# Hybrid decoder layer: spatial layer norm placed behind the recurrence's chunks, branch splits behind the value evictions

## Chip, cores and metric

The kernel runs on one core of one Trainium2 chip. The metric is the device time of one execution in microseconds. The kernel before takes 758.96 us, the median of 3 runs (758.95 to 759.19).

## The reference, cut to what matters

One decoder layer on x (512 tokens, 1024 channels). An RMS norm is followed by one wide input projection w_in whose columns feed three token mixers, their gate paths and the merge gates. The mixers are a sparse attention (NSA), a chunked spatial-gating MLP and an RWKV-7 recurrence. Each mixer's output is multiplied by a SiLU gate, projected from 512 to 1024 channels, scaled by a sigmoid merge gate and summed; an output projection, a gated per-layer embedding and a last RMS norm follow. Everything is float32. The two parts that the change touches:

```python
def _spatial_gating(u, v, ln_g, ln_b, w_s, b_s):
    vn = ((vf - mu) * lax.rsqrt(var + LN_EPS)) * ln_g + ln_b      # layer norm of v over 512 channels
    mixed = einsum('gts,bcsgd->bctgd', tril(w_s), vn) + b_s       # 8 groups, chunks of 128 tokens
    return u * mixed

ys = stack([y_nsa * silu(nz), y_sg * silu(sz), y_rk * silu(rz)])  # the three finished branch outputs
zs = einsum('bsnc,ncd->bsnd', ys, w_branch)
x = x + sum(sigmoid(mg) * zs) @ w_o
```

The recurrence (`_rwkv7`) carries a 64 x 64 state for each of 8 heads over the 512 tokens.

## The kernel before, in words

**Projections in three products.** Each float32 operand of a projection is split into a high part (rounded to the matmul's reduced float32 type) and a low part, and a product is made of three matmuls: high by high, high by low, low by high. `wload` (L66 to L79) brings one piece of weights: a DMA on SP's queue into wr (L75, 4 buffers), a cast on ScalarE into the high half wh (L77, 5 buffers), a subtraction into the low half wl (L78, 5 buffers). The engine of that subtraction is what `ph_["l"]` holds, VectorE or GpSimd, and is set from place to place. A piece holds at most 560 elements per partition, so a block of 128 columns by 1024 rows takes 2 pieces, 256 columns take 4. `fm_block` (L149) makes one block of 128 output features for all 512 tokens, 24 matmuls with 512 columns; `tm_chunk` (L159) makes up to 512 features for four tiles of 128 tokens. Both put their result into the PSUM tile mm_ps, which has two banks (L58), and call an eviction function.

**Order of the work.** The kernel is written as one list; a scheduler of the framework then puts every engine's instructions into an order of its own, by the program's order as priority and by its own timeline of the kernel, and each engine works its list off in that order. `tc.issue_after(ins)` adds an edge: the instructions of the block that run on the engine of `ins` stand behind `ins` in that engine's list. The projections that don't depend on the mixers (su, sv, merge gates, sz, rz, nz) are so laid between the steps of the mixers.

**The recurrence** (L536 to L605) goes over 8 chunks of 64 tokens. In each chunk TensorE makes r_ps from the state SV, ScalarE copies it, TensorE makes u_ps, VectorE and ScalarE copy it into SV (L557, L558), TensorE makes the state update s_ps (st_ps in the trace), VectorE adds and scales it into tn (L567, or L569 and L570) and VectorE and ScalarE copy tn into the next chunk's SV (L572, L573). The next chunk's r_ps reads that. Every second chunk a group norm of the outputs follows (L582 to L605).

**Spatial gating** (L641 to L689). su and sv have been stored to device memory by then. The norm's parameters lng and lnb, the spatial weights, us and vn (sv's tiles) are loaded on SP's queue; for each of four tiles VectorE runs bn_stats and bn_aggr (L665, L666); the inverse deviation rs4 comes from VectorE and GpSimd (L668, L669); then for each tile VectorE subtracts and scales (L671), GpSimd multiplies with lng (L672), VectorE adds lnb (L673). Eight mixing matmuls (mx_ps), the gate product with sz, and four transposes give y1, which is stored to device memory (L689).

**Branch outputs and NSA's projections.** After rz and nz (L691 to L701), y1 is loaded (zs, L724) and split into ysH and ysL by `split` (L715: ScalarE L716, VectorE L717); for y2 the recurrence's output vt is joined with rz (zs, L729; L730) and split in the same way. Then come the projections of NSA: values and gate for four tiles (`ev_v`, L743 to L749: L745 ScalarE, L746 VectorE, L747 ScalarE, L748 VectorE), four query blocks (`ev_q`, L752) and two key blocks (`ev_k`, L761). The attention and the merges (L775) follow; merge 1 is the first to read y1. The merge's tiles (pool gp, L772) take over memory that is released when y2 is done.

```python
    def split(h, l, src, sc):
        S.activation(h, src, AF.Copy, scale=sc)
        V.scalar_tensor_tensor(l, src, sc, f(h), op0=OP.mult, op1=OP.subtract)
```

Of the kernel before, what the change touches and what calls it, by code (L numbers as in the profile page):

```python
# [9 lines left out]
F32 = mybir.dt.float32  # L10
# [21 lines left out]
CH = {("nz", 3): 7, ("nz", 2): 5}  # L32
LV = (("su", 0), ("su", 1), ("sv", 0), ("sv", 1))
C0 = math.exp(-0.5)

# [4 lines left out]
def f(ap):  # L40
    return ap.bitcast(F32)
# [3 lines left out]
def hybrid_kernel(ctx, tc, x, p, norm_g, w_in, cmp_w1, cmp_w2, cmp_pe, sg_ln_g, sg_ln_b, sg_w, sg_b,  # L45
# [489 lines left out]

    canch = []  # L536
    own = [slice(0, 64), slice(64, 128)]
    for c in range(8):
# [20 lines left out]
        if c < 7:  # L559
            s_ps = rps.tile([128, 4, 64], F32, tag="ch", name="st_ps", bufs=2)  # L560
            for q in range(4):
                for e in range(2):
                    mm(s_ps[own[e], q, :], BKt[:, c, q, e, :], SV[:, c, e, q, :], True, True)
            tn = iv.tile([128, 4, 64], F32, tag="tn", name="tn", bufs=2)
            dbc = Dt[:, :, c:c + 1].to_broadcast([128, 4, 64])
            if c == 0:
                V.tensor_tensor(tn, s_ps, dbc, OP.mult)  # L567
            else:
                V.tensor_tensor(tn, s_ps, sn, OP.add)  # L569
                V.tensor_tensor(tn, tn, dbc, OP.mult)  # L570
            sn = tn
            V.tensor_copy(SV[own[0], c + 1, 0], tn[own[0]])  # L572
            S.copy(SV[own[1], c + 1, 1], tn[own[1]])  # L573
# [45 lines left out]
    for m in range(NG):  # L619
# [5 lines left out]
        with ExitStack() as es:  # L625
            if ("sg", m) in CH:
                es.enter_context(tc.issue_after(canch[CH["sg", m]]))
            fm_block(O_MG + 1024 + m * 128, 128, ev_m)

    for nm, off in (("sz", O_SZ),):  # L630
        for hf in range(2):
            def ev_t(t, ps, nm=nm, hf=hf):
# [6 lines left out]
                SY.dma_start(dr[nm][t * 128:(t + 1) * 128, hf * 256:hf * 256 + 256], st[:, 0:256])  # L639
            tm_chunk([(w_in, off + 256 * hf, 256)], hH, hL, 8, ev_t)  # L640
    sg_ctx = ExitStack()  # L641
    sp = sg_ctx.enter_context(tc.tile_pool(name="sp", bufs=2))
# [17 lines left out]
    for t in range(4):  # L660
        rows = slice(t * 128, (t + 1) * 128)
        SY.dma_start(us[:, t, :], dr["su"][rows, :])
        SY.dma_start(vn[:, t, :], dr["sv"][rows, :])
        bs = sp.tile([128, 6], F32, tag="bs", name="bs", bufs=1)
        V.bn_stats(bs, vn[:, t, :])  # L665
        V.bn_aggr(mv[:, t, :], bs)  # L666
    rs4 = sp.tile([128, 4], F32, tag="rs4", name="rs4", bufs=1)
    V.tensor_scalar(rs4, mv[:, :, 1], 1e-5, None, op0=OP.add)  # L668
    G.tensor_tensor(rs4, rs4, mhalf[:, 0:4], OP.pow)  # L669
    for t in range(4):  # L670
        V.tensor_scalar(vn[:, t, :], vn[:, t, :], mv[:, t, 0:1], rs4[:, t:t + 1], op0=OP.subtract, op1=OP.mult)  # L671
        G.tensor_tensor(vn[:, t, :], vn[:, t, :], lng, OP.mult)  # L672
        V.tensor_tensor(vn[:, t, :], vn[:, t, :], lnb, OP.add)  # L673
    for g in range(8):
# [43 lines left out]

    zp_ctx = ExitStack()
    zp = zp_ctx.enter_context(tc.tile_pool(name="zp", bufs=4))  # L720
    y1H, y1L = ytiles()
    for q in range(4):
        zs = zp.tile([128, 512], F32, tag="z", name="zs")
        SY.dma_start(zs, dr["y1"][q * 128:(q + 1) * 128, :])  # L724
        split(y1H[:, q, :], y1L[:, q, :], zs, 0.5)
    y2H, y2L = ytiles()
    for q in range(4):
        zs = zp.tile([128, 512], F32, tag="z", name="zs")
        SY.dma_start(zs, dr["rz"][q * 128:(q + 1) * 128, :])  # L729
        V.scalar_tensor_tensor(vt[:, q, :], vt[:, q, :], pc("lnx_b", q), zs, op0=OP.add, op1=OP.mult)  # L730
        split(y2H[:, q, :], y2L[:, q, :], vt[:, q, :], 0.5)
    zp_ctx.close()
    kp_ctx.close()


# [3 lines left out]
    kst = [nsa.tile([128, 2, 2, 512], R, name=f"kst{b}") for b in range(2)]  # L739
    vst = nsa.tile([128, 4, 2, 2, 128], R, name="vst")  # L740
    gate = nsa.tile([128, 4, 24], F32, name="gate")

    def ev_v(t, ps):  # L743
        pv = ps[:, 0:256].rearrange("p (b g d) -> p b g d", b=2, g=2)
        S.copy(vst[:, t, :, :, 0:64], pv)  # L745
        V.tensor_tensor(vst[:, t, :, :, 64:128], pv, f(vst[:, t, :, :, 0:64]), OP.subtract)  # L746
        S.activation(gate[:, t, :], ps[:, 256:280], AF.Tanh, scale=0.5)  # L747
        V.tensor_scalar(gate[:, t, :], gate[:, t, :], 0.5, 0.5, op0=OP.mult, op1=OP.add)  # L748
    tm_chunk([(w_in, O_NVS, 128), (w_in, O_NVW, 152)], hH, hL, 8, ev_v)  # L749

    for q in range(4):
        def ev_q(ps, q=q):  # L752
            S.activation(qst[0:64, q, 0, :], ps[0:64], AF.Copy, scale=0.125)
            S.activation(qst[64:128, q, 1, :], ps[64:128], AF.Copy, scale=0.125)
            V.scalar_tensor_tensor(qst[64:128, q, 0, :], ps[0:64], 0.125, f(qst[0:64, q, 0, :]),
                                   op0=OP.mult, op1=OP.subtract)
            V.scalar_tensor_tensor(qst[0:64, q, 1, :], ps[64:128], 0.125, f(qst[64:128, q, 1, :]),
                                   op0=OP.mult, op1=OP.subtract)
        fm_block(O_NQ + 128 * q, 128, ev_q)
    for b in range(2):  # L760
# [8 lines left out]
        fm_block((O_NKS, O_NKW)[b], 128, ev_k)  # L769


    gp = ctx.enter_context(tc.tile_pool(name="gp", bufs=2))  # L772
# [224 lines left out]
```

## Time and profile before

| what | value |
|---|---|
| time of the runs, median (lowest to highest) | 758.96 us (758.95 to 759.19) |
| time of the profiled execution | 758.88 us |
| its span from the first to the last instruction | 757.1 us |
| mean granted TensorE clock | 0.989 |
| ScalarE busy | 353.7 us |
| GpSimd busy | 327.6 us |
| DMA | 78.73 MB, mean 104 GB/s |

The profile names engines in short: PE is TensorE's matmuls, PEld its weight loads, DVE VectorE, ACT ScalarE, POOL GpSimd, SP the queue of SyncE. The granted clock is a share of 2.4 GHz. Idle time of an engine is put down to what ended it last. In rows of a timeline the first number is the start, the second the duration, both in us, and the bracket is the idle time ahead of it with its releaser.

### The profile page before, as it was taken

How to read it: one execution, taken by the hardware profiler on the slowest of the kernel's cores; microseconds unless marked ns; L12 is line 12 of the kernel's file. 1: busy time of each engine (PE TensorE's matmuls, PEld its weight loads, DVE VectorE, ACT ScalarE, POOL GpSimd, SP SyncE). 2: the span in 40 equal slices, each digit the busy share in tenths (PEclk: the TensorE clock that was granted, in tenths of full speed). 3: DMA queues.
4: the chain of work that ended last, by engine and by line, in shares of the span. 5: the costliest groups of instructions: out<-in, count | busy, mean ns of one | idle time of the engine just before them, and what ended most of it. 6: DMA issues, size and time to landing. Idle time of an engine off the chain costs nothing.

```text
span 757.1 us, 13075 instructions
## 1 busy us (share of the span) xinstructions
PE 720.5 (95%) x4941; PEld 610.3 (81%) x4941; DVE 403.1 (53%) x747; ACT 353.7 (47%) x743; POOL 327.6 (43%) x304
## 2 busy tenths in 40 slices
PE   4999999999996999999899999989999999999995
PEld 4888788899875987778777777867877888998995
DVE  6531688658817553456558456387655222216335
ACT  6454565533351332334464655476654333127453
POOL 6455731020335343424534335533445656256563
PEclk9999999999998999999999999999999999999999
DMA  5853222234553353346434222211117433222222
GB/s 197 186 142 85 64 73 59 72 97 118 147 171 111 100 165 112 103 140 182 138 84 125 57 56 56 71 29 42 43 47 250 121 98 110 72 98 75 79 70 112
DMA packets 106689, 78.73 MB, mean 104 GB/s; under 512 B 5569, under 2 KB 97282, under 8 KB 106626
## 3 DMA queue, kind: packets, MB, share of 16 engines
q1 hardware_dynamic: 105890, 75.27, 34.6%
q10 hardware_dynamic: 736, 2.63, 0.8%
q8 instruction: 39, 0.64, 0.3%
q14 instruction: 24, 0.20, 0.1%
HBM read 67.91 MB, written 9.96 MB: 103 GB/s over the span
## 4 chain that ended last, share of the span: by engine, by line
PE 83%; DVE 6%; DMA 3%; ACT 3%; issue 2%; POOL 1%; SPq 0%; ACTq 0%; POOLq 0%; DVEq 0%
PE mm_ps L61 66%; PE s_ps L61 3%; PE o_ps L61 2%; PE g_ps L61 2%; PE p_ps L861 2%; PE Yp L61 1%; DMA vn<-dr_sv 1%; DMA lnb<-in_sg_ln_b_dram 1%; PE r_ps L61 1%; DVE mx L847 1%; PE mx_ps L61 1%; DVE vn L671 1%; DVE pl L865 1%; ACT wh L77 1%; DMA zs<-dr_y 1%
## 5 line engine op out<-in xcount | busy, mean ns | idle before, releaser
L78 POOL TENSOR_TENSOR wl<-wr,wh 128x512 fp32r<-128x512 f32 (+1 forms) x168 | 225.0, 1348 | 292.8 <-ACT wh L77 279.1
L77 ACT CAST wh<-wr 128x512 fp32r<-128x512 f32 (+1 forms) x194 | 119.1, 620 | 162.7 <-PE mm_ps L61 112.3
L61 PE MATMUL mm_ps<-hH,wh 128*128 128x512 f32 (+1 forms) x440 | 174.9, 397 | 5.7 <-ACT gate L747 2.8
L61 PE MATMUL mm_ps<-hL,wh 128*128 128x512 f32 (+1 forms) x440 | 172.9, 393 | 0.0
L61 PE MATMUL mm_ps<-hH,wl 128*128 128x512 f32 (+1 forms) x440 | 172.2, 392 | 0.0
L61 PEld LDWEIGHTS mm_ps<-hH,wh 128*128 128x128 f32 x440 | 83.9, 191 | 24.0 <-ACT gate L747 3.5
L61 PEld LDWEIGHTS mm_ps<-hH,wl 128*128 128x128 f32 x440 | 83.8, 191 | 17.9 <-DVE wl L78 0.3
L61 PEld LDWEIGHTS mm_ps<-hL,wh 128*128 128x128 f32 x440 | 84.0, 191 | 16.7 <-issue 0.2
L61 PE MATMUL mm_ps<-wh,hL 128*128 128x256 f32 (+1 forms) x224 | 65.3, 292 | 0.0
L61 PE MATMUL mm_ps<-wl,hH 128*128 128x256 f32 (+1 forms) x224 | 64.7, 289 | 0.0
L61 PE MATMUL mm_ps<-wh,hH 128*128 128x256 f32 (+1 forms) x224 | 64.3, 289 | 0.0
L61 PEld LDWEIGHTS mm_ps<-wh,hH 128*128 128x128 f32 x224 | 42.8, 192 | 1.3 <-issue 0.5
L61 PEld LDWEIGHTS mm_ps<-wh,hL 128*128 128x128 f32 x224 | 43.0, 192 | 0.9 <-issue 0.5
L61 PEld LDWEIGHTS mm_ps<-wl,hH 128*128 128x128 f32 x224 | 42.9, 191 | 0.8
L865 DVE TENSOR_TENSOR pl<-p_ps,ph 128x512 fp32r<-128x512 f32 x40 | 27.1, 684 | 26.8 <-ACT ph L864 26.7
L61 PE MATMUL mm_ps<-ysH,wh 128*128 128x512 f32 x96 | 38.6, 402 | 0.2 <-ACT ysH L716 0.2
L61 PE MATMUL mm_ps<-ysL,wh 128*128 128x512 f32 x96 | 38.4, 400 | 0.2 <-DVE ysL L717 0.2
L61 PE MATMUL mm_ps<-ysH,wl 128*128 128x512 f32 x96 | 38.2, 398 | 0.0
L848 ACT ACTIVATE P<-s_ps,mx 128x512 f32<-128x512 f32 (+3 forms) x64 | 33.4, 532 | 7.8 <-DVE mx L847 5.5
L61 PE MATMUL mm_ps<-wh,mH 128*128 128x256 f32 x128 | 36.1, 286 | 0.6 <-DVE x L910 0.6
L61 PE MATMUL mm_ps<-wl,hT 128*128 128x256 f32 x128 | 35.8, 281 | 0.0
L61 PE MATMUL mm_ps<-wl,mH 128*128 128x256 f32 x128 | 35.8, 281 | 0.0
(336 smaller groups left out, 1437.1 us busy)
## 6 DMA issues: line engine op xcount, KB each, us to landing
wr<-in_w_in_dram SPq DMA_DIRECT2D x130, 256.0 KB
wr<-in_w_branch_dram SPq DMA_DIRECT2D x24, 256.0 KB
wr<-in_w_o_dram SPq DMA_DIRECT2D x16, 256.0 KB
wr<-in_w_ple_gate_dram SPq DMA_DIRECT2D x16, 256.0 KB
xs__129<-in_x_dram SPq DMA_DIRECT2D x4, 512.0 KB
w1t<-in_cmp_w_dram SPq DMA_DIRECT2D x4, 512.0 KB
x<-in_x_dram ACTq DMA_DIRECT2D x4, 512.0 KB
out_dram<-x SPq DMA_DIRECT2D x8, 256.0 KB
```

The lines of the kernel that those rows point to most:

```text
L61: return PE.matmul(o, a, b, start=start, stop=stop, **kw).ins
L77: S.copy(h[:, :m], raw[:, :m])
L78: ph_["l"].tensor_tensor(l[:, :m], raw[:, :m], f(h[:, :m]), OP.subtract)
L671: V.tensor_scalar(vn[:, t, :], vn[:, t, :], mv[:, t, 0:1], rs4[:, t:t + 1], op0=OP.subtract, op1=OP.mult)
L847: V.tensor_reduce(mx[:, hh:hh + 1], s_ps[:, :W], axis=AX.X, op=OP.max, negate=True)
L848: S.activation(P[:, hh, :W], s_ps[:, :W], AF.Exp, bias=mx[:, hh:hh + 1], accum_out=sm[:, hh:hh + 1])
L861: PE.transpose(p_ps[:, hh * 128:hh * 128 + 128], P[:, hh, kt * 128:kt * 128 + 128], ident)
L865: V.tensor_tensor(pl, p_ps, f(ph), OP.subtract)
```

## The change

`vanch` collects VectorE's last state copy of each chunk 0 to 6 (L572). With LA = 1, bn_stats and bn_aggr of all four tiles stand behind chunk 1's copy on VectorE, the norm of tiles 0 and 1 behind chunk 2's, that of tiles 2 and 3 behind chunk 3's. The multiplication with lng moves from GpSimd to VectorE. The low halves of sz's weights, and those of the NSA values, queries and keys, are made on VectorE in place of GpSimd. The loads and splits of y1 and y2 move behind the NSA projections in the program; on ScalarE and VectorE y1's stand behind the gate instructions of value tile 3, and y2's behind the evictions of query blocks 0 (for q = 0, 1) and 1 (for q = 2, 3).

```diff
+LA = 1
-    canch = []
+    canch, vanch = [], []
-            V.tensor_copy(SV[own[0], c + 1, 0], tn[own[0]])
+            vanch.append(V.tensor_copy(SV[own[0], c + 1, 0], tn[own[0]]).ins)
+    ph_["l"] = V
     for nm, off in (("sz", O_SZ),):
...
+    ph_["l"] = G
...
-        V.bn_stats(bs, vn[:, t, :])
-        V.bn_aggr(mv[:, t, :], bs)
+        with tc.issue_after(vanch[LA]):
+            V.bn_stats(bs, vn[:, t, :])
+            V.bn_aggr(mv[:, t, :], bs)
...
-        V.tensor_scalar(vn[:, t, :], vn[:, t, :], mv[:, t, 0:1], rs4[:, t:t + 1], op0=OP.subtract, op1=OP.mult)
-        G.tensor_tensor(vn[:, t, :], vn[:, t, :], lng, OP.mult)
-        V.tensor_tensor(vn[:, t, :], vn[:, t, :], lnb, OP.add)
+        with tc.issue_after(vanch[LA + 1 + t // 2]):
+            V.tensor_scalar(vn[:, t, :], vn[:, t, :], mv[:, t, 0:1], rs4[:, t:t + 1], op0=OP.subtract, op1=OP.mult)
+            V.tensor_tensor(vn[:, t, :], vn[:, t, :], lng, OP.mult)
+            V.tensor_tensor(vn[:, t, :], vn[:, t, :], lnb, OP.add)
...
-    (loads and splits of y1 and y2: from here)
+    nanch = []
+    ph_["l"] = V
...
-        S.activation(gate[:, t, :], ps[:, 256:280], AF.Tanh, scale=0.5)
-        V.tensor_scalar(gate[:, t, :], gate[:, t, :], 0.5, 0.5, op0=OP.mult, op1=OP.add)
+        a_ = S.activation(gate[:, t, :], ps[:, 256:280], AF.Tanh, scale=0.5).ins
+        nanch.append((a_, V.tensor_scalar(gate[:, t, :], gate[:, t, :], 0.5, 0.5, op0=OP.mult, op1=OP.add).ins))
...
+    (ev_q appends its second activation and its last VectorE instruction to nanch in the same way)
...
+    y1H, y1L = ytiles()
+    for q in range(4):
+        zs = zp.tile([128, 512], F32, tag="z", name="zs")
+        SY.dma_start(zs, dr["y1"][q * 128:(q + 1) * 128, :])
+        with tc.issue_after(nanch[3][0]), tc.issue_after(nanch[3][1]):
+            split(y1H[:, q, :], y1L[:, q, :], zs, 0.5)
+    y2H, y2L = ytiles()
+    for q in range(4):
+        zs = zp.tile([128, 512], F32, tag="z", name="zs")
+        SY.dma_start(zs, dr["rz"][q * 128:(q + 1) * 128, :])
+        with tc.issue_after(nanch[4 + q // 2][0]), tc.issue_after(nanch[4 + q // 2][1]):
+            V.scalar_tensor_tensor(vt[:, q, :], vt[:, q, :], pc("lnx_b", q), zs, op0=OP.add, op1=OP.mult)
+            split(y2H[:, q, :], y2L[:, q, :], vt[:, q, :], 0.5)
+    zp_ctx.close()
+    kp_ctx.close()
+    ph_["l"] = G
```

## Rows read from the trace of the kernel before

**Rows 1.** The page, busy us of each engine, share of the span, instructions.

```profile
PE 720.5 (95%) x4941; PEld 610.3 (81%) x4941; DVE 403.1 (53%) x747; ACT 353.7 (47%) x743; POOL 327.6 (43%) x304
```

**Rows 2.** Waits of PE over the span: us in total, times, longest.

```profile
PE r_ps L61 <- DVE SV L572: 3.3, 1, 3.3
PE st_ps L61 <- DVE SV L557: 3.2, 1, 3.2
PE mm_ps L61 <- ACT gate L747: 2.8, 2, 2.0
```

**Rows 3.** Windows: length, busy PE, PEld, DVE, ACT, POOL, granted clock, DMA share, GB/s.

```profile
227.40:230.60 3.20, 0.01 (x1) 0.00 (x0) 1.89 (x5) 0.00 (x0) 0.00 (x0) 1.00 0.71 263
230.60:234.90 4.30, 4.25 (x38) 3.56 (x39) 2.49 (x7) 1.47 (x3) 1.54 (x2) 0.61 0.42 135
237.30:240.60 3.30, 0.02 (x1) 0.03 (x1) 3.27 (x5) 1.02 (x3) 3.30 (x4) 1.00 0.16 55
240.60:245.40 4.80, 4.80 (x51) 4.53 (x51) 3.62 (x5) 1.25 (x3) 4.05 (x2) 0.64 0.14 55
353.50:362.20 8.70, 5.90 (x26) 4.45 (x25) 8.70 (x10) 5.24 (x13) 6.48 (x5) 1.00 0.67 177
```

**Rows 4.** Timeline of DVE, 227 to 240 us.

```profile
227.44 0.69 DVE L665 BATCH_NORM_STATS2 bs<-vn 128x6 f32<-128x512 f32 x1 [10.27 <-DMA vn<-dr_sv]
...
230.20 0.40 DVE L557 COPY SV<-u_ps 64x256 f32<-64x256 f32 x1
...
232.11 0.69 DVE L665 BATCH_NORM_STATS2 bs<-vn 128x6 f32<-128x512 f32 x1 [0.36 <-DMA vn<-dr_sv]
...
234.42 4.78 DVE L671 TENSOR_SCALAR vn<-vn,mv,rs 128x512 f32<-128x512 f32 x4 [1.20 <-POOL rs L669]
239.11 0.41 DVE L567 TENSOR_TENSOR tn<-st_ps,Dt 128x256 f32<-128x256 f32 x1
```

**Rows 5.** Timeline of ACT: one cast, and two gate activations.

```profile
231.52 0.61 ACT L77 CAST wh<-wr 128x512 fp32r<-128x512 f32 x1
...
354.07 0.19 ACT L747 ACTIVATE gate<-mm_ps 128x24 f32<-128x24 f32 x1
...
361.94 0.18 ACT L747 ACTIVATE gate<-mm_ps 128x24 f32<-128x24 f32 x1
```

**Rows 6.** Line L78 by engine: ns shortest/median/longest, first and last start.

```profile
L78 POOL TENSOR_TENSOR wl<-wr,wh x168: 1263/1301/2450, 21.2 to 739.9; 128x512 fp32r<-128x512 f32 x164, 128x560 fp32r<-128x560 f32 x4
...
L78 DVE TENSOR_TENSOR wl<-wr,wh x26: 660/686/1789, 16.7 to 191.1; 128x512 fp32r<-128x512 f32 x26
```

**Rows 7.** Tile vn: its mixing matmuls and the addition of lnb, columns as before.

```profile
L61 PE MATMUL mx_ps<-vn,wsT x16: 379/431/483, 281.0 to 323.2; 128*128 128x256 f32 x16
...
L673 DVE TENSOR_TENSOR vn<-vn,lnb x4: 673/676/1759, 240.4 to 243.4; 128x512 f32<-128x512 f32 x4
```

**Rows 8.** Timeline of SP's queue: a weight load of sz, the branch weights.

```profile
225.99 0.39 SPq L75 DMA_DIRECT2D wr<-in_w_in_dram  x1
...
369.86 14.89 SPq L75 DMA_DIRECT2D wr<-in_w_branch_dram  x6
```

**Rows 9.** Timeline of PE after the second stop.

```profile
240.60 0.69 PE L61 MATMUL r_ps<-SV,Gt 128*64 128x64 f32 x16 [3.28 <-DVE SV L572]
...
241.62 0.48 PE L61 MATMUL mm_ps<-wl,hH 128*128 128x256 f32 x1
```

**Rows 10.** Chain that ended last: start, us, what.

```profile
225.15 6.86 DMA vn<-dr_sv
...
353.62 2.72 DMA zs<-dr_rz
...
368.02 5.64 PE mm_ps L61 x24
```

**Rows 11.** Window in the attention, columns as in rows 3.

```profile
480.00:560.00 80.00, 74.37 (x419) 59.17 (x418) 54.16 (x132) 49.25 (x136) 32.09 (x27) 0.99 0.17 44
```

More of the change, by code (lines that the diff above doesn't have):

```diff
@@ L717, in split @@
         V.scalar_tensor_tensor(l, src, sc, f(h), op0=OP.mult, op1=OP.subtract)
[L719 to L733, printed above, removed]
     nsa_ctx = ExitStack()
@@ L753, in ev_q @@
             S.activation(qst[0:64, q, 0, :], ps[0:64], AF.Copy, scale=0.125)
-            S.activation(qst[64:128, q, 1, :], ps[64:128], AF.Copy, scale=0.125)
+            a_ = S.activation(qst[64:128, q, 1, :], ps[64:128], AF.Copy, scale=0.125).ins
             V.scalar_tensor_tensor(qst[64:128, q, 0, :], ps[0:64], 0.125, f(qst[0:64, q, 0, :]),
                                    op0=OP.mult, op1=OP.subtract)
-            V.scalar_tensor_tensor(qst[0:64, q, 1, :], ps[64:128], 0.125, f(qst[64:128, q, 1, :]),
-                                   op0=OP.mult, op1=OP.subtract)
+            nanch.append((a_, V.scalar_tensor_tensor(qst[0:64, q, 1, :], ps[64:128], 0.125, f(qst[64:128, q, 1, :]),
+                                                     op0=OP.mult, op1=OP.subtract).ins))
         fm_block(O_NQ + 128 * q, 128, ev_q)
@@ L769, in hybrid_kernel @@
         fm_block((O_NKS, O_NKW)[b], 128, ev_k)
+    zp_ctx = ExitStack()
+    zp = zp_ctx.enter_context(tc.tile_pool(name="zp", bufs=4))
+    y1H, y1L = ytiles()
[14 more added lines that the diff above has]
+    ph_["l"] = G
     gp = ctx.enter_context(tc.tile_pool(name="gp", bufs=2))
```

## The prediction

> **What bounds the kernel now.** I read the page's busy line first: TensorE is busy for 720.5 of 757.1 us [rows 1]. So the time is TensorE's own work plus 36.6 us in which it stands still, plus what it does at the lower clock. A change that adds no matmul can win only there. Next I read who TensorE waits for [rows 2]. Three rows lie where the diff edits. r_ps waits once, 3.3 us, for the state copy of L572. st_ps waits once, 3.2 us, for the state copy of L557. mm_ps waits twice, 2.8 us in all, for the gate activation of L747. The other long waits of that list stand in the first 40 us or in the attention, which the diff does not edit. Then I cut the span into stretches around these waits [rows 3]. From 227.4 to 230.6 and from 237.3 to 240.6 TensorE does nothing (0.01 and 0.02 us). The 4.3 us after the first stop have a granted clock of 0.61, the 4.8 us after the second 0.64: most of each is spent at 1.2 GHz in place of 2.4. From 353.5 to 362.2 TensorE works 5.90 of 8.70 us, VectorE all 8.70, and the clock stays at 1.00.
>
> Why the copies are late is in VectorE's timeline [rows 4]. It takes its instructions in the order of its queue. The first bn_stats of the layer norm stands ahead of chunk 0's copy of u_ps into SV, and sits idle for 10.27 us until the load of vn lands. The copy starts at 230.20, behind the second bn_stats. The four subtract-and-scale instructions (234.42, 4.78 us) then hold chunk 0's state update tn until 239.11. So TensorE's two stops are one thing: the layer norm is ahead of the recurrence in VectorE's queue, and one of its loads is late.
>
> The third stop is in the queues of ScalarE and VectorE [rows 5]. The gate activations of tiles 2 and 3 run at 354.07 and 361.94. Between them stand splits of the finished branch outputs (L716 on ScalarE, L717 and L730 on VectorE). Both banks of mm_ps are full until a gate activation has read its bank.
>
> **The change, part by part.** 1. The norm behind the chunks. bn_stats goes behind chunk 1's state copy, tiles 0 and 1 of the norm behind chunk 2's, tiles 2 and 3 behind chunk 3's. Both stops go: 3.24 and 3.28 us. With them goes the low clock: at full clock the columns of 4.3 us at 0.61 take 2.62 us, those of 4.8 us at 0.64 take 3.07 us, so 1.68 + 1.73 = 3.4 us. Part 1 is worth 3.2 + 3.3 + 3.4 = 9.9 us. The ends of the clock term are 0 (if the low clock stays for another reason) and 3.4; I take 3.4, since both low stretches follow such a stop and no other stretch near them is low. bn_stats no longer finds its data missing: without the stops chunk 1 does not begin before 232 (part 3), and the last bn_stats had its data at 232.11 [rows 4].
>
> What is late next? The norm's result. The eight mixing matmuls need it, and in the trace they begin at 281.0, some 36 us after the last addition of the norm (from 243.4) [rows 7]; that slack covers a norm that comes up to two chunks later.
>
> 2. Its multiplications on VectorE: four of 128x512 leave GpSimd. The nearest row is the addition of the same shape on VectorE, 676 ns [rows 7]: 2.7 us more there. They lie behind a chunk's last copy, while TensorE runs the matmuls of sz, rz and nz that stand between the chunks' steps. Cost nothing; without that cover 2.7 us.
>
> 3. The low halves of the weights on VectorE: 8 loads of sz, 4 of the values and 12 of queries and keys, 24 splits. They take 1.30 us each on GpSimd and 0.69 on VectorE [rows 6], so 31 us leave GpSimd and 16.6 join VectorE, which is busy for 53% of the span [rows 1]. The durations are hidden; the place in the queue is the danger. A split waits for ScalarE's cast, the cast for the load, and the recurrence's copies now stand in the same queue. The one load to look at is the fourth of sz. It is issued at 225.99 [rows 8], behind the norm's loads, and cast at 231.52 [rows 5]. TensorE's work between the two stops lasts 6.7 us in the trace and 6.7 - 1.7 = 5.0 at full clock, so without the first stop it is through at 227.4 + 5.0 = 232.4. The next matmul after the stop, at 241.62, is one with a low half of sz [rows 9]. In the bad end that half is ready at 231.52 + 0.61 + 0.69 = 232.8 plus what the copies need; in the good end the load lands early and it is ready before 232.
>
> What the load takes: the last load of vn, issued 0.8 us earlier, took 6.86 us to land, a load of zs of the same 256 KB in a quieter stretch 2.72 us [rows 10]. I take the late end, as it is of the same place, bounded by the cast: 0.4 us of wait, and 0.4 more for the split's place in the queue, 0.8 us given back (ends 0 and 3.9, see the first rival).
>
> The Trainium skill, page "DMA: Bandwidth & Descriptors", section on the anatomy of one DMA, gives a transfer on GpSimd's path about 2.0 us plus its bytes at 436 GB/s, an estimate of 2.6 us for 256 KB. By it nothing is given back; the vn row, 6.86 us behind other loads, disagrees, the zs row agrees.
>
> 4. The branch splits behind the evictions: y1 (4 loads, 4 splits) now comes behind the last gate, y2 behind the first and second query block. The gate activations no longer stand behind splits: 2.8 us [rows 2] come back; the clock did not fall there, so nothing more. On ScalarE and VectorE the splits now lie beside the query blocks, each 5.64 us on TensorE [rows 10]. Their results are wanted only when the merge of branch 1 begins, after all the query and key blocks. On SP the 8 loads are moved behind 20 transfers of weights, and the gate tiles' loads, which take over the released memory, come later too. wh and wl have 5 buffers each, so TensorE has up to 5 loads of weights ahead. Cost nothing while that lead holds; without it, see the slower rival.
>
> **Sum.** 9.9 + 2.8 - 0.8 = 11.9 us. The profiled execution lasted 758.88 us, 0.08 under the median of 758.96: 758.9 - 11.9 = 747.0 us.
>
> One more unknown: the order of all later work is found anew, by a scheduler that the diff feeds with other priorities. From 480 to 560 us, in the attention, TensorE works 74.37 of 80 us [rows 11], 5.6 us of idle. With no row for another order I take 0, and half of it, 2.8 us, either way for the range.
>
> **Rivals.** A. A weight split takes the norm's place: chunk 0's update tn (due at 228.5) stands behind the fourth sz split until 232.8. From tn to r_ps it took 1.5 us [rows 4, 9], so r_ps starts at 234.3 in place of 232.4: 1.9 us of stop, and up to 1.7 of low clock after it, 3.6 more than the full gain, with 0.3 for the next copies 3.9: 758.9 - 12.7 + 3.9 = 750.1 us. For it: the load really is cast late. Against it: VectorE's order may well put tn first.
>
> B. The loads land quickly: 758.9 - 12.7 = 746.2 us. For it the zs row, against it the vn row.
>
> C. The order does not do what it says: the edges only fix what comes first, and if another instruction with a late load (the norm's parameters, a sz split) heads VectorE's queue at chunk 0, both stops remain, and only the 2.8 us are won: 756.1 us. Against it: every instruction that waited there is moved behind an edge.
>
> D. Slower. The 8 loads of y1 and y2 on SP. If they are queued behind the train of branch weights (issuing six took 14.89 us [rows 8]), ScalarE stands at the first y1 split, and with it the casts and the query evictions. TensorE then fills its two banks, one block of 5.64 us, and stops: 14.89 + 2.72 - 5.64 = 12.0 us, and 1.7 of low clock. That is 13.7 against a gain of 11.9: 760.7 us. It decides from the point at which the loads land 5.64 + 10.2 = 15.8 us after ScalarE reaches the split. For it: these loads now come after all the weights in the program. Against it: the splits are held back as well, by the value evictions and by up to two query blocks.
>
> **How the numbers follow.** The forecast of 747.0 has 0.45, B 0.17, A 0.20, C 0.07, D 0.08; 0.03 is left for no change. With the unknown order of 2.8 us the forecast and B reach from 743.4 to 749.8, A to 752.9. The range is 743.4 to 753.0 and leaves out C, D and no change, 0.18. About 0.2%, 1.5 us, is what a measurement of this kernel can tell from no change. Faster by more: 0.45 + 0.17 + 0.20 + 0.07 = 0.89, less 0.01 for C with a bad order, 0.88; within: 0.03 + 0.01 = 0.04; slower 0.08.
>
> **What would show it.** Right: r_ps, st_ps and mm_ps wait for L572, L557 and L747 no more, the clock is 1.00 from 227 on, bn_stats is idle for less than 1 us and starts after 235. A: VectorE idle before L78 for the cast, with r_ps waiting behind. B: no such wait. C: the old waits under another releaser. D: ScalarE idle before the split of L716 for a load of zs, with mm_ps waiting. Wrong altogether: TensorE's idle between 200 and 400 us falls as forecast and the total does not, because it comes back in the attention.

## The result and the profile after

The changed kernel takes 746.65 us, the median of 5 runs (745.82 to 748.49), beside 758.96 (757.54 to 759.39, 5 runs) for the kernel before on the same chip: a ratio of 0.9843, 95% interval 0.9829 to 0.9858. The forecast was 747.0. The profiled execution lasted 747.35 us, its span 745.6, against 758.88 and 757.1.

In the changed kernel a line that stood at L61 is at L62, L557 at L558, L567 at L568, L572 at L573, L665 at L669, L671 at L676, L687 at L692 and L747 at L739; L673's addition is at L678.

The page, busy time of each engine, answers to [rows 1]:

```profile
PE 716.0 (96%) x4941; PEld 606.6 (81%) x4941; DVE 407.6 (55%) x775; ACT 354.2 (48%) x743; POOL 288.2 (39%) x276
```

GpSimd is relieved by 39 us and VectorE is busy for only 4.5 more, although 28 instructions of about 0.69 us, 19 us in all, came to it: others of its instructions became shorter (last section). TensorE has the same 4941 matmuls and is busy with them for 4.5 us less; its mean granted clock is 0.993 in place of 0.989. The other 7 us are time in which it no longer stands still. TensorE's waits, answering to [rows 2]:

```profile
PE ut_ps L692 <- DVE us L688: 1.3, 1, 1.3
...
PE r_ps L62 <- DVE SV L573: 0.4, 1, 0.4
```

The three rows on which the prediction stood are gone: st_ps and the gate's mm_ps are not in the list, and the r_ps row of 3.3 us has become one of 0.4 at another place. A row that the prediction did not name is there: ut_ps, the transposes behind the gate product, waits once for 1.3 us. The windows, answering to [rows 3] and [rows 11]:

```profile
227.40:240.00 12.60, 12.60 (x176) 11.28 (x174) 3.21 (x8) 3.03 (x7) 0.00 (x0) 1.00 0.62 216
...
318.00:320.00 2.00, 0.85 (x16) 0.54 (x12) 2.00 (x5) 0.37 (x1) 0.00 (x0) 1.00 0.25 65
320.00:322.00 2.00, 1.47 (x14) 1.18 (x15) 0.68 (x3) 0.99 (x2) 0.00 (x0) 0.90 0.72 242
322.00:324.00 2.00, 2.00 (x25) 1.52 (x23) 0.00 (x0) 0.96 (x2) 0.00 (x0) 0.50 0.36 133
...
340.00:360.00 20.00, 20.00 (x108) 17.31 (x107) 14.67 (x26) 12.10 (x24) 0.00 (x0) 1.00 0.65 194
480.00:560.00 80.00, 74.59 (x415) 59.34 (x414) 55.97 (x140) 48.84 (x135) 30.40 (x27) 0.98 0.17 46
```

Where TensorE stood still for two times 3.2 us and ran at 0.61 and 0.64 it now works without a gap at full clock, and the gate's stretch (340 to 360) is full too. The new dent is at 318 to 324, with a granted clock of 0.50, the lower of its two levels, from 322 to 324. The attention's window has 5.4 us of idle, where it had 5.6. VectorE's timeline after, answering to [rows 4]:

```profile
226.98 0.69 DVE L79 TENSOR_TENSOR wl<-wr,wh 128x512 fp32r<-128x512 f32 x1 [2.36 <-ACT wh L78]
228.59 0.42 DVE L568 TENSOR_TENSOR tn<-st_ps,Dt 128x256 f32<-128x256 f32 x1 [0.93 <-PE st_ps L62]
...
241.26 0.68 DVE L669 BATCH_NORM_STATS2 bs<-vn 128x6 f32<-128x512 f32 x1
```

tn comes at 228.59, not 239.11. bn_stats comes at 241.26 and has its data (no bracket, so no idle ahead of it). A weight split stands just ahead of tn and does not delay it: tn waits for st_ps alone.

**A measure that the experiments need.** Medians of these kernels, built from four to thirteen runs, can differ by 1 to 2 us for reasons outside the edit (last section). So I also cut each trace at three matmuls. The first iv_ps comes ahead of the recurrence; the last r_ps ends its chain; the first s_ps opens the attention's scores, behind all that the diff moves. Stretch A is from the first iv_ps to the last r_ps, stretch B from there to the first s_ps. The rows for it, by tile, of the kernel before and of the changed one (the last pair of times is the first and the last start):

```profile
L61 PE MATMUL iv_ps<-itmp,Gt x128: 191/191/212, 206.1 to 208.1; 32*32 32x32 f32 x128
...
L61 PE MATMUL r_ps<-SV,Gt x128: 222/222/270, 212.8 to 331.8; 128*64 128x64 f32 x128
...
L61 PE MATMUL s_ps<-kst,qst x128: 220/338/481, 390.9 to 559.3; 128*128 128x512 f32 x32, 128*128 128x384 f32 x32, 128*128 128x256 f32 x32, 128*128 128x128 f32 x32
```

```profile
L62 PE MATMUL iv_ps<-itmp,Gt x128: 191/191/212, 206.5 to 208.5; 32*32 32x32 f32 x128
...
L62 PE MATMUL r_ps<-SV,Gt x128: 222/222/369, 213.2 to 323.2; 128*64 128x64 f32 x128
...
L62 PE MATMUL s_ps<-kst,qst x128: 218/338/481, 379.8 to 548.8; 128*128 128x512 f32 x32, 128*128 128x384 f32 x32, 128*128 128x256 f32 x32, 128*128 128x128 f32 x32
```

Before, A is 331.8 - 206.1 = 125.7 us and B 390.9 - 331.8 = 59.1; after, 116.7 and 56.6. The gain in A + B is 11.5 us, the whole of the profiled execution's 758.88 - 747.35 = 11.5. A and B stand for one profiled execution of each kernel; one kernel that was profiled twice differs by 1.6 us in A (e3 and e10 below).

### The profile page after: what moved, and what is told of

The parts are those of the page before. It is cut to its first block, busy times and chain, and to the rows that moved or that the text cites. A ratio compares the mean times of both kernels' runs of the same rounds, so it can differ in the third digit from the quotient of the medians.

```text
span 745.6 us, 13074 instructions
## 1 busy us (share of the span) xinstructions
PE 716.0 (96%) x4941; PEld 606.6 (81%) x4941; DVE 407.6 (55%) x775; ACT 354.2 (48%) x743; POOL 288.2 (39%) x276
## 4 chain that ended last, share of the span: by engine, by line
PE 87%; DVE 5%; ACT 2%; issue 2%; DMA 1%; POOL 1%; SPq 1%; ACTq 0%; POOLq 0%; DVEq 0%
PE mm_ps L62 69%; PE s_ps L62 3%; PE o_ps L62 2%; PE g_ps L62 2%; PE p_ps L872 2%; DMA w1t<-in_cmp_w_dram 1%; PE Yp L62 1%; PE r_ps L62 1%; DVE mx L858 1%; PE st_ps L62 1%; PE mx_ps L62 1%; DVE pl L876 1%; PE u_ps L62 1%; PE bk_ps L477 1%; ACT wh L78 1%
## 5 line engine op out<-in xcount | busy, mean ns | idle before, releaser
L79 POOL TENSOR_TENSOR wl<-wr,wh 128x512 fp32r<-128x512 f32 x144 | 192.5, 1345 | 276.5 <-ACT wh L78 255.5
L78 ACT CAST wh<-wr 128x512 fp32r<-128x512 f32 (+1 forms) x194 | 119.4, 620 | 169.6 <-PE mm_ps L62 117.6
L62 PE MATMUL mm_ps<-hH,wh 128*128 128x512 f32 (+1 forms) x440 | 174.2, 396 | 3.8 <-ACT kc L265 2.3
L62 PE MATMUL mm_ps<-hL,wh 128*128 128x512 f32 (+1 forms) x440 | 171.1, 389 | 0.0
L62 PE MATMUL mm_ps<-hH,wl 128*128 128x512 f32 (+1 forms) x440 | 170.7, 388 | 0.4 <-DVE wl L79 0.4
L62 PEld LDWEIGHTS mm_ps<-hH,wh 128*128 128x128 f32 x440 | 82.9, 188 | 21.3 <-ACT kc L265 2.5
L62 PEld LDWEIGHTS mm_ps<-hH,wl 128*128 128x128 f32 x440 | 82.7, 188 | 18.0 <-DVE wl L79 0.6
L62 PEld LDWEIGHTS mm_ps<-hL,wh 128*128 128x128 f32 x440 | 83.0, 189 | 16.5 <-issue 0.2
L62 PE MATMUL mm_ps<-wh,hL 128*128 128x256 f32 (+1 forms) x224 | 64.9, 290 | 0.0
L62 PE MATMUL mm_ps<-wh,hH 128*128 128x256 f32 (+1 forms) x224 | 63.8, 286 | 0.0
L62 PE MATMUL mm_ps<-wl,hH 128*128 128x256 f32 (+1 forms) x224 | 63.6, 285 | 0.0
L79 DVE TENSOR_TENSOR wl<-wr,wh 128x512 fp32r<-128x512 f32 (+1 forms) x50 | 38.0, 769 | 25.2 <-ACT wh L78 25.1
L62 PEld LDWEIGHTS mm_ps<-wh,hL 128*128 128x128 f32 x224 | 42.2, 188 | 1.1 <-issue 0.5
L62 PEld LDWEIGHTS mm_ps<-wh,hH 128*128 128x128 f32 x224 | 42.0, 188 | 1.2 <-issue 0.5
L62 PEld LDWEIGHTS mm_ps<-wl,hH 128*128 128x128 f32 x224 | 42.2, 188 | 0.5
L62 PE MATMUL mm_ps<-ysH,wh 128*128 128x512 f32 x96 | 38.6, 402 | 0.1
L62 PE MATMUL mm_ps<-ysL,wh 128*128 128x512 f32 x96 | 38.4, 400 | 0.2 <-DVE ysL L722 0.2
L62 PE MATMUL mm_ps<-ysH,wl 128*128 128x512 f32 x96 | 38.2, 398 | 0.0
L62 PE MATMUL mm_ps<-wh,mH 128*128 128x256 f32 x128 | 36.1, 286 | 0.6 <-DVE x L921 0.6
L62 PE MATMUL mm_ps<-wl,hT 128*128 128x256 f32 x128 | 35.9, 281 | 0.0
```

Source lines behind the costliest of these rows:

```text
L62: return PE.matmul(o, a, b, start=start, stop=stop, **kw).ins
L78: S.copy(h[:, :m], raw[:, :m])
L79: ph_["l"].tensor_tensor(l[:, :m], raw[:, :m], f(h[:, :m]), OP.subtract)
```

## The experiments

All kernels in one table; "before" is the median of the kernel before on the same chip. A and B are in us, from the same three rows of each trace.

| kernel | median (runs) | before | ratio, 95% | A | B |
|---|---|---|---|---|---|
| e1_norm_order | 749.92 (4) | 757.85 | 0.9883 (0.9853 to 0.9913) | 115.3 | 61.3 |
| e2_branch_order | 755.72 (10) | 757.85 | 0.9968 (0.9955 to 0.9981) | 126.0 | 55.7 |
| e3_order_both | 745.44 (4) | 757.85 | 0.9829 (0.9805 to 0.9852) | 116.9 | 55.8 |
| e4_engines_only | 752.48 (4) | 757.85 | 0.9921 (0.9890 to 0.9953) | 120.1 | 57.0 |
| e9_change | 747.17 (4) | 758.63 | 0.9855 (0.9841 to 0.9870) | 116.6 | 57.9 |
| e10_order_both | 745.42 (5) | 758.63 | 0.9832 (0.9817 to 0.9848) | 115.3 | 55.8 |
| e7_values_pool | 746.99 (4) | 758.63 | 0.9848 (0.9835 to 0.9862) | 116.3 | 58.1 |
| e11_sz_pool | 743.23 (4) | 758.63 | 0.9803 (0.9790 to 0.9817) | 114.9 | 55.8 |
| e5_la0 | 743.56 (4) | 758.50 | 0.9798 (0.9780 to 0.9817) | 115.1 | 55.8 |
| e6_la3 | 743.55 (4) | 758.50 | 0.9796 (0.9780 to 0.9813) | 112.2 | 58.4 |
| e8_vn_first | 755.96 (7) | 758.50 | 0.9965 (0.9949 to 0.9981) | 122.3 | 58.7 |
| e12_z_buffer | 743.00 (5) | 758.50 | 0.9798 (0.9778 to 0.9818) | 114.6 | 55.8 |

### The change taken apart

Two theories. Order: the gain comes from what stands ahead of what in the queues. Relief: it comes from taking work off GpSimd, whose instructions slow VectorE's. The first four kernels make one part of the change alone, or all parts but one kind. e1 has the edges of the norm alone:

```diff
+        with tc.issue_after(vanch[LA]):
             V.bn_stats(bs, vn[:, t, :])
             V.bn_aggr(mv[:, t, :], bs)
...
+        with tc.issue_after(vanch[LA + 1 + t // 2]):
             V.tensor_scalar(vn[:, t, :], vn[:, t, :], mv[:, t, 0:1], rs4[:, t:t + 1], op0=OP.subtract, op1=OP.mult)
             G.tensor_tensor(vn[:, t, :], vn[:, t, :], lng, OP.mult)
             V.tensor_tensor(vn[:, t, :], vn[:, t, :], lnb, OP.add)
```

> Two theories. Order: the gain is the place of instructions in VectorE's and ScalarE's queues. Relief: the gain is that 28 instructions leave GpSimd, which stretches VectorE's instructions beside it. This kernel is the one before with the layer norm's order edges alone (bn_stats behind chunk 1's copy, the norm behind chunks 2 and 3); every engine assignment and the branch splits are as before. Order expects 758.96 - 9.9 = 749.1 us (748 to 751), the waits of r_ps and st_ps for VectorE gone, the two waits of mm_ps for the gate still there with 2.8 us. Relief expects 758 to 759 us.

Measured: 749.92 us, 7.9 under before; A fell by 10.4 us. The waits of r_ps and st_ps are gone, and 227.4 to 246 is full at clock 1.00. B grew by 2.2 us. The gate's wait is still there, and a low clock is now behind it. e1, TensorE's wait and the windows around the gate's second stop:

```profile
PE mm_ps L62 <- ACT gate L756: 3.0, 2, 2.1
```

```profile
346.00:350.00 4.00, 4.00 (x18) 3.00 (x16) 4.00 (x4) 2.30 (x5) 3.85 (x3) 1.00 0.62 148
350.00:354.00 4.00, 1.95 (x5) 1.48 (x5) 4.00 (x5) 2.81 (x6) 2.20 (x3) 0.78 0.45 122
354.00:358.00 4.00, 4.00 (x15) 3.19 (x14) 3.26 (x5) 0.62 (x1) 1.89 (x2) 0.79 0.29 78
```

e2 moves the loads and splits of y1 and y2 alone, as the change does, with the engines and the norm as before:

```diff
-    (loads and splits of y1 and y2: ahead of the NSA projections)
+    (loads and splits of y1 and y2: behind them, under the edges of nanch)
```

> The kernel before with the branch outputs' loads and splits moved behind the value and query evictions, nothing else: the norm and every engine assignment as before. Order expects 758.96 - 2.8 = 756.2 us (755.5 to 757), the gate waits gone, both stops near the recurrence's first chunks as before (3.2 and 3.3 us). Relief expects 758 to 759 us.

Measured: 755.72 us, 2.1 under before. B fell by 3.4 us and the gate's wait is gone; A is as before (126.0). The stops of r_ps and st_ps remain, with 4.8 and 2.3 us.

e3 has both orders, with every multiplication and weight split on the engine that it had before:

```diff
-            V.tensor_tensor(vn[:, t, :], vn[:, t, :], lng, OP.mult)
+            G.tensor_tensor(vn[:, t, :], vn[:, t, :], lng, OP.mult)
-    ph_["l"] = V
+    ph_["l"] = G
```

(against the changed kernel; the second edit at sz and at the NSA projections)

> Both orders as in the change, but the norm's multiplications and all 24 weight splits on GpSimd as before. Order expects the time of the change, 746.7 us (745.5 to 748), and that the sum of the two single runs' gains is this one's, 12.7 us. Relief expects 757 us or more, since no instruction has left GpSimd.

Measured: 745.44 us, 12.4 under before. The two orders alone give all of the gain. The same kernel ran again later beside the change on one chip:

> Both orders with all engine assignments as before, once more, now beside the change on one chip. Values expects 1 to 1.5 us less than the change, as the value splits are on GpSimd here too; None expects the same time within 0.7 us.

Measured: 745.42 us, 13.2 under before and 1.75 under the change, and A + B 171.1 us, 13.7 under before.

e4 is the counterpart, the engines of the change in the old order:

```diff
-        G.tensor_tensor(vn[:, t, :], vn[:, t, :], lng, OP.mult)
+        V.tensor_tensor(vn[:, t, :], vn[:, t, :], lng, OP.mult)
+    ph_["l"] = V
```

(against the kernel before; the last line at sz, with G again behind it, and at the NSA projections)

> The engine moves alone: the norm's multiplications and the 24 splits on VectorE, order of the norm and of the branch splits as before. Order expects 754 to 759 us: the norm still stands ahead of the recurrence and waits for vn, so a stop of about 3 us at st_ps stays; the second stop may shorten by up to 2.6 us, since four subtract-and-scale instructions took 4.78 us beside GpSimd and take about 0.5 us each without it. Relief expects 746 to 749 us.

Measured: 752.48 us, 5.4 under before, between the two theories' numbers. Its trace is of its fastest run, 749.17 us, so its A and B are some 3 us better than its median. The stops are shorter, 2.0 us at st_ps and 1.4 us in two waits of r_ps, and the clock of 227 to 246 is 1.00, where it was 0.82. VectorE's timeline in e4:

```profile
233.34 1.92 DVE L674 TENSOR_SCALAR vn<-vn,mv,rs 128x512 f32<-128x512 f32 x4 [0.91 <-POOL rs L672]
...
235.77 0.42 DVE L568 TENSOR_TENSOR tn<-st_ps,Dt 128x256 f32<-128x256 f32 x1
```

The four subtractions that took 4.78 us [rows 4] take 1.92 with no instruction of GpSimd beside them, and tn comes at 235.77 in place of 239.11. So Relief is a real effect: it shortens what stands in tn's way. Once nothing stands there it is worth nothing: e3 and e10 have the full gain without it. Relief falls as the cause of the change's gain.

### What gives part of it back: the stop at chunk 7

The changed kernel is slower than its orders alone, and has the stop at 318 to 324. I first suspected the splits of the value weights (the wl of 128x560), one of which stands on VectorE just ahead of the late instructions. e9 is the change itself, run beside the others:

> The changed kernel itself, on the same chip as the next three. Expected 746 to 747 us. In its trace TensorE stops 1.3 us at ut_ps and 0.4 us at r_ps around 320 us, and then runs at a granted clock of 0.50 from 322 to 324. Two theories for that. Values: a low-half split of the NSA value weights, waiting for its cast, stands on VectorE ahead of chunk 6's update tn and the gate product that ut_ps needs. None: such a stop comes with any order of this stage (the kernel before stops there 0.7 us) and engine assignments do not matter.

e7 puts the value splits back, e11 those of sz:

```diff
 (e7)
-    ph_["l"] = V                (at the NSA projections; V again from the query blocks on)
+    ph_["l"] = G
 (e11)
-    ph_["l"] = V                (at sz)
+    ph_["l"] = G
```

> The change with the 4 low-half splits of the NSA values on GpSimd again, the rest of the change kept (sz, queries and keys and the norm's multiplications on VectorE). Values expects the stop at 320 us to shrink to the 0.7 us of the kernel before and the clock to stay at 1.00: 1 us of stop and some 1.7 us of low clock less, 744 to 745.5 us. None expects the time of the change within 0.7 us.

> The change with the 8 low-half splits of sz on GpSimd again, the rest kept. My prediction gave 0.8 us back for the fourth of these splits; in the trace of the change it runs at 226.98, before tn at 228.59, and no wait follows. So both theories of the last run expect the time of the change within 0.7 us; 0.8 us or more below it would bear out the term of the prediction.

Measured: e9 747.17, e7 746.99, e11 743.23 us. e7 still has a wait of 1.1 us at ut_ps and a clock of 0.71 in 318 to 326, so the value splits are not it. e11 came out 3.9 us under the change, so None falls too: the engine of a split does matter. By the sign I had written down, 0.8 us or more, e11 would bear out the prediction's term for the fourth sz split; the traces put the loss elsewhere. The stop of 1.3 us and the low clock are gone. One window of e9 and the same of e11:

```profile
318.00:326.00 8.00, 6.33 (x63) 4.78 (x62) 2.56 (x7) 2.53 (x5) 0.00 (x0) 0.71 0.39 134
```

```profile
318.00:326.00 8.00, 6.97 (x87) 5.39 (x86) 4.06 (x11) 3.61 (x8) 0.00 (x0) 1.00 0.57 202
```

The splits of sz are made from 216 to 246. What is different at 318 is in VectorE's timelines, first of e9, then of e11:

```profile
317.27 0.74 DVE L79 TENSOR_TENSOR wl<-wr,wh 128x560 fp32r<-128x560 f32 x1 [0.45 <-ACT wh L78]
317.93 0.42 DVE L570 TENSOR_TENSOR tn<-st_ps,tn 128x256 f32<-128x256 f32 x1
318.26 0.68 DVE L701 SCALAR_TENSOR_TENSOR st<-st,mm_ps 128x512 f32<-128x512 f32 x1
318.86 0.68 DVE L688 TENSOR_TENSOR us<-us,z 128x512 f32<-128x512 f32 x1
319.46 0.42 DVE L571 TENSOR_TENSOR tn<-tn,Dt 128x256 f32<-128x256 f32 x1
319.91 0.28 DVE L573 COPY SV<-tn 64x256 f32<-64x256 f32 x1
```

```profile
317.07 0.69 DVE L688 TENSOR_TENSOR us<-us,z 128x512 f32<-128x512 f32 x1 [1.20 <-DMA z<-dr_sz]
...
318.33 0.41 DVE L570 TENSOR_TENSOR tn<-st_ps,tn 128x256 f32<-128x256 f32 x1
```

The gate products of the spatial branch (L688) come 1.6 us later in e9: the first of them starts at 314.93 there and at 313.33 in e11. In e9 the fourth product stands inside the last state update (chunk 6's, which chunk 7 starts from), between L570 and L571, and in e11 ahead of it.

No wait carries this delay from 246 to 313. One window of e9 and the same of e11:

```profile
222.00:316.00 94.00, 94.00 (x908) 79.06 (x904) 52.66 (x115) 30.66 (x62) 28.90 (x20) 1.00 0.50 145
```

```profile
222.00:316.00 94.00, 94.00 (x902) 79.14 (x903) 48.35 (x110) 30.77 (x62) 35.81 (x26) 1.00 0.49 146
```

TensorE is busy without a gap at full clock in both. What differs is the order of its list: between the starts of chunks 3 and 4 stand 65 projection matmuls in e9 and 61 in e11, between those of chunks 6 and 7 it is 27 and 33, and in all chunks together 406 in both. The first mixing matmul starts at 275.1 in e9 and at 271.6 in e11. So the delay comes with another order, which the scheduler found when the splits' engine was changed, and not with a split that somebody waits for. TensorE's timeline shows what that costs; e9, then e11:

```profile
317.79 0.55 PE L692 MATMUL ut_ps<-ident,us 128*128 128x128 f32 x3
319.60 0.33 PE L692 MATMUL ut_ps<-ident,us 128*128 128x128 f32 x1 [1.26 <-DVE us L688]
320.35 0.30 PE L62 MATMUL r_ps<-SV,Gt 128*64 128x64 f32 x2 [0.42 <-DVE SV L573]
...
327.59 0.73 PE L62 MATMUL mm_ps<-hH,wh 128*128 128x512 f32 x1
```

```profile
319.11 0.66 PE L692 MATMUL ut_ps<-ident,us 128*128 128x128 f32 x4 [0.68 <-ACT vn L693]
320.05 0.33 PE L62 MATMUL r_ps<-SV,Gt 128*64 128x64 f32 x2 [0.28 <-DVE SV L573]
...
324.30 0.50 PE L62 MATMUL mm_ps<-hH,wh 128*128 128x512 f32 x1
```

In e9 the stops of 1.26 and 0.42 us follow one another, and from r_ps to the next projection TensorE then needs 327.59 - 320.35 = 7.24 us; in e11 it is 324.30 - 320.05 = 4.25. Of the difference of 2.99, four transposes (0.66 us in e11) are work that e11 has done ahead of r_ps; the other 2.3 us are the lower clock, on small matmuls. The stops are 1.68 us in e9 and 0.96 in e11, 0.7 more; with these 2.3 that is 3.0 of the 3.8 us by which A + B differ (174.5 and 170.7).

Does the wait of 1.2 us for z matter, which e11 still has? In e12 sz's fourth tile gets a buffer of its own, so its load need not wait until the first is read:

```diff
+    z1 = sp.tile([128, 512], F32, tag="z1", name="z1", bufs=1)
-        zs = (z0, lng, lnb, z0)[t]
+        zs = (z0, lng, lnb, z1)[t]
```

(on top of e11)

> The change with sz's splits on GpSimd, and a buffer of its own for the fourth tile of sz, so that its load need not wait until the first tile's product has been read. In the run with sz on GpSimd that product waited 1.2 us for its load, with tn behind it, and TensorE stopped for 0.68 us at ut_ps and 0.28 us at r_ps. If the load sets that stop: 742.3 us, 0.3 to 1 us below that run's 743.2. If ScalarE's copy of ut_ps sets it: the same 743.2.

Measured: 743.00 us, as e11. The wait for z is gone, the wait of 0.7 us for ScalarE's copy of the transposes is there as before, and the load does not set that stop.

### The place of the norm, and the late load

Two theories on part 1. Place: what costs is that the norm stands ahead of the recurrence's copies. Late load: what costs is that vn's loads land late, and loads issued earlier would do as well. e5 and e6 move the norm one chunk forward and two back in the changed kernel; e8 keeps the old order and issues vn's four loads first on SP.

```diff
 (e5)
-LA = 1
+LA = 0
 (e6)
-LA = 1
+LA = 3
 (e8, against the kernel before)
+    for t in range(4):
+        SY.dma_start(vn[:, t, :], dr["sv"][t * 128:(t + 1) * 128, :])
     lng = sp.tile([128, 512], F32, tag="lng", name="lng", bufs=1)
...
-        SY.dma_start(vn[:, t, :], dr["sv"][rows, :])
```

> The kernel before with one edit: the four loads of vn are issued ahead of lng, lnb, the spatial weights and us on SP's queue. The norm still stands ahead of the recurrence on VectorE. Place expects that the first stop (3.2 us, bn_stats waiting) shrinks or goes and that the second remains at about 2 us, since the four subtract-and-scale instructions of 4.78 us still hold tn: 750 to 755 us. Late load expects both stops gone, with their low clock: 749 us or less.

Measured: 755.96 us, 2.5 under before. VectorE's timeline in e8, and TensorE's wait:

```profile
227.20 0.41 DVE L557 COPY SV<-u_ps 64x256 f32<-64x256 f32 x1
228.48 4.85 DVE L672 TENSOR_SCALAR vn<-vn,mv,rs 128x512 f32<-128x512 f32 x4 [0.87 <-POOL rs L670]
233.26 3.41 DVE L674 TENSOR_TENSOR vn<-vn,lnb 128x512 f32<-128x512 f32 x2
236.59 0.41 DVE L567 TENSOR_TENSOR tn<-st_ps,Dt 128x256 f32<-128x256 f32 x1
```

```profile
PE r_ps L61 <- DVE SV L572: 5.3, 1, 5.3
```

With the loads early the first stop is gone (the copy comes at 227.20, not 230.20), and the second has grown from 3.3 to 5.3 us: subtractions and additions now stand ahead of tn together. A fell by 3.4 of the 10.4 us that e1 has. Late load, with 749 us or less, falls; the place is what costs. Place's own 750 to 755 us were missed by 1 us, because the second stop grew where it was to shrink to 2 us.

> The change with LA = 0: bn_stats behind chunk 0's state copy, the norm's tiles behind chunks 1 and 2. The last load of vn lands near 232, chunk 0's copy is at 229, so bn_stats meets missing data again, but no state copy of chunk 0 stands behind it. Place (the norm costs only where it stands ahead of a due copy) expects the time of the change within 1 us, with bn_stats idle for 1 to 3 us and no wait of st_ps or r_ps over 0.5 us. Late load (a bn_stats that finds its data missing costs, wherever it stands) expects a stop of 2 us or more at chunk 1 and 749 us or more.

> The change with LA = 3: bn_stats behind chunk 3's copy, the norm behind chunks 4 and 5. My prediction said that the slack before the mixing matmuls covers a norm up to two chunks later. The mixing matmuls begin at 276 in the change and, eight of them in turn, are spread to 314; here the norm ends near 305. If the slack holds, 746 to 748 us. If the chain mixing, gate product, transposes, store and load of y1 is then late, VectorE and TensorE wait after the last chunk: 749 to 756 us. I expect the second, at about 751.

Measured: 743.56 and 743.55 us, both 15 under before, where e9 was 11.5 under. For e5 Place had the time of the change within 1 us, and for e6 I had expected a loss; both came out some 3.5 us faster. In e5 bn_stats runs from 230.39, directly behind chunk 0's copy, with its data there, so e5 is no test of Late load; e8 is. In e6 the norm's last addition is at 305.8 and the first mixing matmul at 307.4, in place of 273.9 and 275.6 in the changed kernel, and the last transposes fall behind chunk 7, under the projections. Neither has the wait of 1.3 us at ut_ps, and the clock of 312 to 326 is 1.00 in both. e6's wait of 1.3 us is at another matmul:

```profile
PE mx_ps L62 <- DVE us L682: 1.3, 1, 1.3
```

So the stop at chunk 7 is a meeting of two things, the gate products and the last state update. It is avoided by having the products come earlier (e5, e11) or later (e6); the engine of sz's splits is only one of the things that shift them.

## Why the prediction was right, and where not

**Part 1, the norm behind the chunks: 9.9 us forecast, 10.4 measured** (A of e1, 125.7 - 115.3; the difference is less than the 1.6 us by which A varies). Both stops and both low stretches went, as forecast. That the low clock would go with the stops held: 227 to 246 is at 1.00 in e1 and after. The claim that a later norm costs nothing at the mixing held, but not by the slack of 36 us: the mixing matmuls begin at 275.6 in the changed kernel, 1.7 us behind the start of the last addition, with no wait, and e6 puts the norm two chunks later still, where the mixing moves along (307.4) and nothing is lost.

**Part 2, the multiplications on VectorE: nothing forecast.** e10 has them on GpSimd, e11 on VectorE (with the splits of the NSA weights), and A + B is 171.1 and 170.7 us. Held, to within 0.4 us. The effect that I did not price, shorter subtractions on VectorE, is worth up to 5.4 us in the old order (e4, which moves the splits too) and none in the new.

**Part 3, the weight splits on VectorE: -0.8 us at the fourth sz split. Here the step failed, in place, cause and size.** At that split there is no loss: in the changed kernel ScalarE's cast came at 226.32 and VectorE's split at 226.98, not 231.52 and after. The prediction had taken the cast at 231.52 for a load that lands late, and that reading was wrong twice. The load issued at 225.99 is not this one: wr has four buffers, and a load goes out as the subtraction four pieces earlier ends. The fourth sz load so went out at 217.36, and the one of 225.99 is the sixth, cast at 252.62. And the cast was late because ScalarE stood ahead of it, 7.15 us at its own state copy, which the first stop held up; the cast [rows 5] follows with no idle ahead of it. SP's timeline and ScalarE's in the kernel before:

```profile
217.36 0.39 SPq L75 DMA_DIRECT2D wr<-in_w_in_dram  x1
```

```profile
230.63 0.37 ACT L558 COPY SV<-u_ps 64x256 f32<-64x256 f32 x1 [7.15 <-DVE SV L557]
```

So the term was sized on a delay that part 1 takes away. Instead, with these splits on VectorE the gate products of 315 us come 1.6 us later, into the last state update: 2.6 us by A + B of the profiled changed kernel (173.3 - 170.7), 3.8 by e9 (174.5 - 170.7), 3.9 by the medians of e9 and e11. As it comes with another order of TensorE's list, it belongs to the unknown order that the prediction put at 0 for want of a row, with 2.8 us either way. No row of the kernel before had shown it: ut_ps L687 waited only for ScalarE there. The term's ends, 0 to 3.9 us, happen to hold that cost, but they were worked out for another place.

**Part 4, the branch splits behind the evictions: 2.8 us forecast, 3.4 measured** (B of e2; 3.1 by A + B, 2.1 by the medians). "The clock did not fall there, so nothing more" is true of the kernel before and not of a kernel with part 1 alone: in e1 the same wait (3.0 us) brings windows at 0.78 and 0.79. So the parts do not simply add: 7.9 and 2.1 us apart by medians, 12.4 together; the intervals, some 2 us either way for e1 and e3 and 1 for e2, leave part of that difference open.

**The sum.** 10.4 + 3.4 = 13.8 us, against 13.7 for both orders in e10, less 2.6 to 3.8, is 10.0 to 11.2. A + B fell by 11.5 us in the changed kernel's profile and by 10.3 in e9; the forecast was 11.9, the medians have 12.3 and 11.5. So the mechanism of parts 1 and 4 was right and each came out half a microsecond above the forecast, while what stands for part 3 took 2 to 3 us more than forecast. That the forecast lies within 0.35 us of the median is therefore in part luck: its errors go against one another, and 1 to 2 us lie within what executions of one kernel differ by.

**The rivals.** A (a split takes the norm's place): not at chunk 0; that the loss at chunk 7 has nearly its size is chance. B (the loads land quickly): right that the fourth sz split brings no wait, and its 746.2 us is as near to the result as the forecast, but not for its reason, as that load went out at 218.13, 8.2 us ahead of its cast; what it left out is the stop at chunk 7. C falls: no old wait remains. D falls: in the changed kernel SP issues y1's loads at 338, between two batches of weights and 9 us before ScalarE's splits begin, and these splits have no idle ahead of them. SP's timeline and ScalarE's:

```profile
338.01 1.76 SPq L768 DMA_DIRECT2D zs<-dr_y  x4
344.83 2.96 SPq L76 DMA_DIRECT2D wr<-in_w_in_dram  x4
```

```profile
346.96 2.20 ACT L721 ACTIVATE ysH<-zs 128x512 fp32r<-128x512 f32 x4
```

What stays open: e11, e12, e5 and e6 lie within 0.6 us of one another, and whether e5's or e6's place together with e11's engine gives more was not tried.

## What to carry to other kernels

When the bound engine waits for a short copy on another engine, look at what stands ahead of that copy in its queue: moving the norm behind it gave more (7.9 us by the medians, e1) than making its instructions shorter (5.4 us, e4) or its loads earlier (2.5 us, e8), and with both orders in place (e10) neither was needed for the full gain. Where a scheduler orders the queues, compare the bound engine's order before and after an instruction is moved to another engine, and not only the place it came from: here the loss came at the recurrence's last chunk, some 70 us behind the last of the moved splits. Where an order is right by a few microseconds, try it a step earlier and a step later; both neighbours of this one (743.6 us) beat it.

## What the runs showed that was not expected

- **The same stop can leave the clock up or down.** Before, the gate's second stop of 2 us left the granted clock at 1.00 ([rows 3], and the row below); in e1 the same stop comes with 0.78 and 0.79. Around e9's stops of 1.26 and 0.42 us, among small matmuls, it is 0.71, around e11's of 0.68 and 0.28 us 1.00. And e3 and e10 are one kernel: from 216 to 230, with TensorE busy for 14.00 of 14.00 us in both, e3 has 0.88 and e10 1.00, which is 14 x 0.12 = 1.7 us, the difference of their A (116.9 and 115.3). The windows of the kernel before, behind its gate's stop, and of e3:

```profile
362.00:376.00 14.00, 13.83 (x61) 11.32 (x62) 7.26 (x9) 6.57 (x13) 8.36 (x6) 1.00 0.49 144
```

```profile
216.00:230.00 14.00, 14.00 (x169) 11.15 (x161) 1.39 (x3) 5.82 (x11) 6.46 (x5) 0.88 0.81 258
```

- **Part of a median is outside the edit.** The changed kernel's own two profiles differ so at the attention's end: 0.84 from 540 to 550 in the first, 1.00 in e9. e10 needs 197.9 us from its last s_ps to the end of its span, e11 196.3, with nothing edited there; that is 1.6 of the 1.8 us between their profiled executions (744.88 and 743.12).
- **GpSimd beside VectorE.** The subtract-and-scale of 128x512 takes 532 to 541 ns in the changed kernel and 535 to 1503 ns before, where it lies beside GpSimd's weight split and multiplications. By tile vn, the kernel before:

```profile
L671 DVE TENSOR_SCALAR vn<-vn,mv,rs x4: 535/1486/1503, 234.4 to 237.7; 128x512 f32<-128x512 f32 x4
```

The price can also fall on the other side. In the changed kernel two of them run from 268.33 (0.99 us for both) beside a split on GpSimd, and the split is the one that is longer, 2.31 us where another took 1.29. GpSimd's timeline after:

```profile
248.37 1.29 POOL L79 TENSOR_TENSOR wl<-wr,wh 128x512 fp32r<-128x512 f32 x1
...
268.18 2.31 POOL L79 TENSOR_TENSOR wl<-wr,wh 128x512 fp32r<-128x512 f32 x1 [2.14 <-ACT wh L78]
```

The Trainium skill, page "SBUF — State Buffer", section "Who interferes with whom", says that such an instruction of VectorE can take ports that it shares with GpSimd, and that whichever comes first holds them for its whole length. The trace agrees in kind: the split is longer by 1.02 us, about the length of the two instructions beside it. Who came first it does not settle: the split's row starts at 268.18, ahead of both, and other instructions of VectorE with two inputs lie beside it from 269.24 on.
